# Weight slots 256 bytes longer with an offset per kind of product, and the rotary swap in the common temporaries

## The chip, the cores and the metric

The kernel runs on one core of one Trainium2 chip. The metric is device time in microseconds (us) of one execution. Before the change it takes 2052.59 us, the median of three runs (2052.55 to 2052.70).

## The reference

A decoder trunk of two layers over 512 positions and a width of 2,048, in float32: first an attention layer with compressed, selected and sliding-window keys (NSA, 16 heads of 128 in 4 key groups), then a gated linear recurrence (HGRN2, 16 heads of 128). Each layer is

```
h = rmsnorm(x, norm_w[layer])
proj = h @ w_in                      # all inputs of the mixer, and z
x = x + (mixer(proj) * silu(z)) @ w_out
```

and a last RMSNorm follows. Queries and three kinds of keys get a rotary embedding on the first 32 of 128 dimensions:

```
rot = concat([t1 * cos - t2 * sin, t2 * cos + t1 * sin])   # 16 + 16 dimensions
```

The input projections are 2,048 by 7,216 in the first layer and 2,048 by 8,192 in the second; both output projections are 2,048 by 2,048.

## The kernel before

Every large product is done in three matmuls: each operand is split into a rounded high part (fp32r) and the rest, and high x high, high x low and low x high are summed in PSUM. `split` (L75) does it: ScalarE (ACT) writes the high part, VectorE (DVE) subtracts it from the value. The normed input, transposed, stays in SBUF as `hhi` and `hlo`: 128 partitions by 16 tiles (kt) of 512 positions. Weights are loaded from HBM as `raw` tiles of 128 x 1,024 floats (three buffers) by SyncE's queue and split into `whi` and `wlo` slots of 128 x 512 floats (2,048 bytes per partition, four buffers each) by `split_weights` (L86).

Five kinds of product use them. A matmul has an operand that is loaded into the array first (the weight load, PEld in the profile) and one that streams through it (PE):

- `proj` (L102): 128 columns of weights are loaded, `hhi` or `hlo` streams with 512 positions; 48 matmuls for each of 92 calls, L110 to L112.
- `proj_pair` (L115): two such projections in two halves of 256 positions; the second one's weights go into slots with the tags `ohi` and `olo`. Called twice.
- `proj_rows` (L134): `hhi` and `hlo` are loaded, weights stream with 256 columns, L156 to L158.
- `out_proj` (L161): the split mixer output (`ohi`, `olo`, four buffers each) is loaded, weights stream with 512 columns, L176 to L178.
- `out_proj_half` (L182): the same with 256 columns, L196 to L198.

The last output projection (`last_out_proj`, L388) keeps its weights in `hhi` and `hlo` and streams them. `gates` (L497) has one small projection of its own with `whi` slots.

Tiles come from pools. Where they lie in SBUF follows from the order of the pools and from the tiles' sizes: first `consts` (with x_all, hhi, hlo, eps, ident, nw, four tiles of 16 floats and `gw`), then `weights` (raw, whi, wlo, ohi, olo), then `work`, and behind these the tiles of each layer. A tile with a tag takes the next of that tag's buffers and waits until the tile that was there has been read for the last time. `rope` (L433) copies a projection out of PSUM into a tile with the tag `tmp` (three buffers, shared with the normed rows, the z gates and others), and works on its first 32 partitions with a second tile `sw`, which has a buffer of its own: a shuffle of 32 partitions by 16, two products, and a sum, all on DVE, 28 times in all (16 queries, 12 keys). The order of instructions on each engine is set by a planner that runs a timeline of its own over the program. The PSUM accumulators of the products rotate through two banks.

Of the kernel before, what the change touches and what calls it, by code (L numbers as in the profile page):

```python
# [9 lines left out]
F32 = mybir.dt.float32  # L10
F32R = mybir.dt.float32r
# [7 lines left out]
S = 512  # L19
# [32 lines left out]
class Trunk:  # L52
# [25 lines left out]
        eng = self.nc.gpsimd if on_pool else self.nc.vector  # L78
        eng.tensor_tensor(out=lo, in0=x, in1=hi.bitcast(F32), op=ALU.subtract)  # L79

    def load_split(self, ap, shape, tags=("whi", "wlo"), share=False):
        raw = self.wpool.tile(shape, F32, name="raw", tag="raw")
        self.nc.sync.dma_start(raw, ap)
        return self.split_weights(raw, tags, share)

    def split_weights(self, raw, tags=("whi", "wlo"), share=False):  # L86

        _, nk, cols = raw.shape
        parts, step = [], 512 // cols
        for k0 in range(0, nk, step):  # L90
            n = min(step, nk - k0)
            hi, lo = (self.wpool.tile([128, n, cols], F32R, name=t, tag=t, bufs=4) for t in tags)
            self.split(raw[:, k0:k0 + n, :], hi, lo, share and k0)
            parts += [(hi[:, k, :], lo[:, k, :]) for k in range(n)]
        return parts
# [19 lines left out]
    def proj_pair(self, w, ca, cb):  # L115

        mm = self.nc.tensor.matmul
        units = []
        for c0, tags in ((ca, ("whi", "wlo")), (cb, ("ohi", "olo"))):
            parts = []  # L120
            for c in range(2):
                src = w[c * 1024:(c + 1) * 1024, c0:c0 + 128].rearrange("(k p) n -> p k n", p=128)
                parts += self.load_split(src, [128, 8, 128], tags)
            units.append((self.pproj.tile([128, S], F32, name="acc", tag="acc"), parts))
        for half in range(2):
            ts = slice(half * 256, (half + 1) * 256)
            for acc, parts in units:
                for kt, (hi, lo) in enumerate(parts):
                    mm(acc[:, ts], hi, self.hhi[:, kt, ts], start=kt == 0, stop=False)
                    mm(acc[:, ts], hi, self.hlo[:, kt, ts], start=False, stop=False)  # L130
                    mm(acc[:, ts], lo, self.hhi[:, kt, ts], start=False, stop=kt == KT - 1)
        return units[0][0], units[1][0]

    def proj_rows(self, w, c0, c1):  # L134

        accs = [self.pproj.tile([128, S], F32, name="acc", tag="acc").rearrange("p (t n) -> p t n", t=2)
                for _ in range(2)]
        for c in range(2):
            parts = []
            for r0 in range(c * 1024, (c + 1) * 1024, 512):  # L140
                raw = self.wpool.tile([128, 4, 2, 128], F32, name="raw", tag="raw")
                if c1 == c0 + 128:
                    src = w[r0:r0 + 512, c0:c0 + 256].rearrange("(k p) (b n) -> p k b n", p=128, b=2)
                    self.nc.sync.dma_start(raw, src)
                else:
                    for b, cb in enumerate((c0, c1)):
                        self.nc.sync.dma_start(raw[:, :, b, :],
                                               w[r0:r0 + 512, cb:cb + 128].rearrange("(k p) n -> p k n", p=128))
                parts += self.split_weights(raw.rearrange("p k b n -> p k (b n)"))
            for i, acc in enumerate(accs):  # L150
                for k, (hi, lo) in enumerate(parts):
                    kt = c * 8 + k
                    first, last = kt == 0, kt == KT - 1
                    for t in range(2):
                        ts = slice((2 * i + t) * 128, (2 * i + t + 1) * 128)
                        self.nc.tensor.matmul(acc[:, t, :], self.hhi[:, kt, ts], hi, start=first and t == 0, stop=False)  # L156
                        self.nc.tensor.matmul(acc[:, t, :], self.hhi[:, kt, ts], lo, start=False, stop=False)  # L157
                        self.nc.tensor.matmul(acc[:, t, :], self.hlo[:, kt, ts], hi, start=False, stop=last and t == 1)  # L158
        return [acc.rearrange("p t (b n) -> p t b n", b=2) for acc in accs]
# [22 lines left out]
    def out_proj_half(self, w, h0, og, tiles, then):  # L182

        nc = self.nc
        n = len(og)
        for e in range(8):
            es = slice(e * 256, (e + 1) * 256)
            src = w[h0 * 128:(h0 + n) * 128, es].rearrange("(k p) n -> p k n", p=128)
            parts = self.load_split(src, [128, n, 256], share=True)
            for t0 in tiles[::2]:  # L190
                acc = self.pproj.tile([128, S], F32, name="acc", tag="acc").rearrange("p (t n) -> p t n", t=2)
                for t in range(2):
                    ts = slice((t0 + t) * 128, (t0 + t + 1) * 128)
                    for k, (hi, lo) in enumerate(parts):
                        ohi, olo = (o[:, ts] for o in og[k])
                        nc.tensor.matmul(acc[:, t, :], ohi, hi, start=k == 0, stop=False)  # L196
                        nc.tensor.matmul(acc[:, t, :], ohi, lo, start=False, stop=False)
                        nc.tensor.matmul(acc[:, t, :], olo, hi, start=False, stop=k == n - 1)  # L198
                xs = self.x_all[:, t0:t0 + 2, es]
                nc.vector.tensor_tensor(out=xs, in0=acc, in1=xs, op=ALU.add)  # L200
                if e % 2:
                    then(t0, e // 2)
                    then(t0 + 1, e // 2)
# [229 lines left out]
    def rope(self, acc, q):  # L433
        nc = self.nc
        nc.scalar.copy(q, acc)
        sw = self.work.tile([64, S], F32, name="sw", tag="sw", bufs=1)
        nc.vector.stream_shuffle(sw[32:], q[:32], [(i + 16) % 32 for i in range(32)])
        nc.vector.tensor_tensor(out=sw[:32], in0=sw[32:], in1=self.rt[32:64], op=ALU.mult)
        nc.vector.tensor_tensor(out=q[:32], in0=q[:32], in1=self.rt[:32], op=ALU.mult)
        nc.vector.tensor_tensor(out=q[:32], in0=q[:32], in1=sw[:32], op=ALU.add)  # L440
# [56 lines left out]
    def gates(self, w_in):  # L497

        nc = self.nc
        n = 3 * N_HEADS  # L500

        acc = self.pproj.tile([128, S], F32, name="acc", tag="acc")
        for c in range(2):
            raw = self.wpool.tile([128, 8, n], F32, name="raw", tag="raw")
            nc.sync.dma_start(raw, w_in[c * 1024:(c + 1) * 1024, NSA_GL:NSA_Z].rearrange("(k p) n -> p k n", p=128))
            for k0 in (0, 4):
                w = self.wpool.tile([128, 4, 128], F32R, name="whi", tag="whi", bufs=4)
                self.split(raw[:, k0:k0 + 4, :], w[:, :, :n], w[:, :, n:2 * n])
                for k in range(4):
                    kt = c * 8 + k0 + k  # L510
                    both = lambda: nc.tensor.matmul(acc[:2 * n], w[:, k, :2 * n], self.hhi[:, kt, :],
                                                    start=kt == 0, stop=kt == KT - 1)
                    if kt == 0:
                        both()
                    nc.tensor.matmul(acc[:n], w[:, k, :n], self.hlo[:, kt, :], start=False, stop=False)
                    if kt:
                        both()
        gs = self.work.tile([128, S], F32, name="gs", tag="tmp", bufs=3)
        nc.scalar.copy(gs[:2 * n], acc[:2 * n])
        p = self.ptr.tile([128, 4, 128], F32, name="pt", tag="pt")  # L520
        for j in range(NT):
            nc.tensor.transpose(p[:, j, :2 * n], gs[:2 * n, j * 128:(j + 1) * 128], self.ident[:2 * n, :2 * n])
        nc.vector.tensor_copy(self.gate, p[:, :, :n])
        nc.vector.tensor_tensor(out=self.gate, in0=self.gate, in1=p[:, :, n:2 * n], op=ALU.add)
        nc.scalar.activation(self.gate, self.gate, AF.Sigmoid)
# [206 lines left out]
    def lower_bounds(self, tmp):  # L732

        nc, pool = self.nc, self.consts
# [5 lines left out]
        nc.vector.tensor_tensor(out=e, in0=e, in1=r, op=ALU.mult)  # L740
        nc.vector.tensor_tensor(out=self.lb, in0=e, in1=e, op=ALU.subtract)
        nc.vector.tensor_scalar(self.oml, self.lb, -1.0, 1.0, op0=ALU.mult, op1=ALU.add)
        self.gw = pool.tile([128, 1], F32, name="gw")
        nc.sync.dma_start(self.gw, self.hgrn_gnorm_w.rearrange("l p -> p l"))

    def level_tiles(self, pool):
# [302 lines left out]
```

## Time and profile before

| | |
|---|---|
| median of 3 runs | 2052.59 us |
| the profiled execution | 2051.99 us, of which span 2050.0 us |
| PE, PEld busy | 2019.4 us (99%), 1761.0 us (86%) |
| DVE, ACT, POOL busy | 1252.3 us (61%), 892.0 us (44%), 79.2 us (4%) |
| matmuls | 11,410 |
| the load queue of weights | 29.9% of 16 engines' time |

The span is that of one execution on the chip. PE is TensorE's matmuls and PEld its weight loads, which lie beside the matmuls. A row of a group shows the mean duration of one instruction; matmuls are pipelined, so one's duration reaches into the next, and the pace is read from the starts in the timeline.

### The profile page before, as it was taken

What the parts mean: (1) busy time and instruction counts of PE and PEld (TensorE: products, weight loads), DVE (VectorE), ACT (ScalarE), POOL (GpSimd) and SP (SyncE); (2) the same over time, 40 slices, a digit from 0 to 9 for tenths busy, and PEclk for the clock granted to TensorE, in tenths of its full rate; (3) what the DMA queues carried; (4) which work ended last, traced back from release to release, by engine and by line L of the source; (5) the groups of instructions that cost most, each with busy time, mean ns of one, the idle gap of its engine ahead of it and who ended that gap; (6) DMA issues with size and microseconds to landing.
All of it is one profiled execution on the core that took longest, in us unless ns stands there. A gap on an engine that the chain in (4) does not pass through costs nothing.

```text
span 2050.0 us, 29987 instructions
## 1 busy us (share of the span) xinstructions
PE 2019.4 (99%) x11410; PEld 1761.0 (86%) x11410; DVE 1252.3 (61%) x2944; ACT 892.0 (44%) x1966; POOL 79.2 (4%) x63
## 2 busy tenths in 40 slices
PE   7999999999999999999999999999999999999997
PEld 7789889888988889888998989789897898978885
DVE  7634676565757565756874757457574565645755
ACT  5323554444535353445743444334342344423454
POOL 5000000000000000001300000000000000000004
PEclk9999999999999999999999999999999999999999
DMA  5354222323232323232422232232222323223233
GB/s 166 84 137 110 72 67 68 93 64 91 63 93 64 93 70 93 62 83 83 146 78 87 73 93 69 83 104 74 84 74 91 93 72 93 73 82 97 74 98 114
DMA packets 272673, 179.81 MB, mean 88 GB/s; under 512 B 8192, under 2 KB 254320, under 8 KB 272528
## 3 DMA queue, kind: packets, MB, share of 16 engines
q1 hardware_dynamic: 272528, 177.88, 29.9%
q8 instruction: 90, 1.47, 0.3%
q14 instruction: 55, 0.45, 0.1%
HBM read 173.66 MB, written 4.19 MB: 87 GB/s over the span
## 4 chain that ended last, share of the span: by engine, by line
PE 94%; DVE 3%; issue 1%; ACT 1%; DMA 0%; SPq 0%; DVEq 0%
PE acc L110 16%; PE acc L112 16%; PE acc L111 16%; PE acc L176 4%; PE acc L158 4%; PE acc L156 4%; PE acc L177 4%; PE acc L157 4%; PE acc L178 4%; PE pt L665 2%; PE lv L960 1%; PE lv L936 1%; PE sc L693 1%; PE sc L691 1%; PE ov L673 1%; PE ov L672 1%
## 5 line engine op out<-in xcount | busy, mean ns | idle before, releaser
L77 ACT CAST whi<-raw 128x512 fp32r<-128x512 f32 x612 | 375.2, 618 | 664.2 <-PE acc L111 459.6
L79 DVE TENSOR_TENSOR wlo<-raw,whi 128x512 fp32r<-128x512 f32 x592 | 409.8, 700 | 384.0 <-ACT whi L77 363.8
L112 PE MATMUL acc<-hhi,wlo 128*128 128x512 f32 x1472 | 581.4, 395 | 0.0
L110 PE MATMUL acc<-hhi,whi 128*128 128x512 f32 x1472 | 580.2, 394 | 0.0
L111 PE MATMUL acc<-hlo,whi 128*128 128x512 f32 x1472 | 578.5, 393 | 0.0
L112 PEld LDWEIGHTS acc<-hhi,wlo 128*128 128x128 f32 x1472 | 276.7, 188 | 57.8
L111 PEld LDWEIGHTS acc<-hlo,whi 128*128 128x128 f32 x1472 | 276.6, 188 | 57.5
L110 PEld LDWEIGHTS acc<-hhi,whi 128*128 128x128 f32 x1472 | 276.8, 188 | 55.9
L156 PE MATMUL acc<-whi,hhi 128*128 128x256 f32 x768 | 216.2, 283 | 0.0
L158 PE MATMUL acc<-whi,hlo 128*128 128x256 f32 x768 | 215.7, 281 | 0.0
L157 PE MATMUL acc<-wlo,hhi 128*128 128x256 f32 x768 | 215.4, 281 | 0.0
L176 PE MATMUL acc<-whi,ohi 128*128 128x512 f32 x416 | 160.7, 394 | 6.3 <-DVE zz L1009 3.9
L177 PE MATMUL acc<-wlo,ohi 128*128 128x512 f32 x416 | 163.7, 394 | 0.0
L178 PE MATMUL acc<-whi,olo 128*128 128x512 f32 x416 | 163.0, 392 | 0.0
L157 PEld LDWEIGHTS acc<-wlo,hhi 128*128 128x128 f32 x768 | 145.0, 189 | 0.2
L158 PEld LDWEIGHTS acc<-whi,hlo 128*128 128x128 f32 x768 | 144.7, 188 | 0.1
L156 PEld LDWEIGHTS acc<-whi,hhi 128*128 128x128 f32 x768 | 144.1, 188 | 0.8
L180 DVE TENSOR_TENSOR x_all<-acc,x_all 128x512 f32<-128x512 f32 x112 | 77.0, 689 | 84.9 <-PE acc L178 84.5
L176 PEld LDWEIGHTS acc<-whi,ohi 128*128 128x128 f32 x416 | 78.0, 188 | 25.0 <-DVE zz L1009 5.4
L714 ACT ACTIVATE p<-p,nm 128x512 f32<-128x512 f32 (+3 forms) x128 | 71.3, 557 | 55.9 <-DVE nm L711 55.3
L177 PEld LDWEIGHTS acc<-wlo,ohi 128*128 128x128 f32 x416 | 78.1, 188 | 17.9 <-DVE wlo L79 3.0
L178 PEld LDWEIGHTS acc<-whi,olo 128*128 128x128 f32 x416 | 78.1, 188 | 15.9
(272 smaller groups left out, 2881.1 us busy)
## 6 DMA issues: line engine op xcount, KB each, us to landing
raw<-in_hgrn_w_in_dram SPq DMA_DIRECT2D x128, 512.0 KB, 4.1
raw<-in_nsa_w_in_dram SPq DMA_DIRECT2D x96, 512.0 KB, 3.8
raw<-in_nsa_w_out_dram SPq DMA_DIRECT2D x40, 512.0 KB, 3.8
raw<-in_hgrn_w_out_dram SPq DMA_DIRECT2D x32, 512.0 KB, 3.8
raw<-in_nsa_w_in_dram SPq DMA_DIRECT2D x32, 256.0 KB, 3.4
out_dram<-x_all SPq DMA_DIRECT2D x16, 256.0 KB, 2.7
x_all<-in_x_dram SPq DMA_DIRECT2D x6, 512.0 KB, 8.8
raw<-in_nsa_ck_w_dram SPq DMA_DIRECT2D x4, 512.0 KB, 4.0
```

The costliest lines, as they stand in the source:

```text
L77: self.nc.scalar.copy(hi, x)
L79: eng.tensor_tensor(out=lo, in0=x, in1=hi.bitcast(F32), op=ALU.subtract)
L110: self.nc.tensor.matmul(acc, hi, self.hhi[:, kt, :], start=first, stop=False)
L111: self.nc.tensor.matmul(acc, hi, self.hlo[:, kt, :], start=False, stop=False)
L112: self.nc.tensor.matmul(acc, lo, self.hhi[:, kt, :], start=False, stop=last)
L156: self.nc.tensor.matmul(acc[:, t, :], self.hhi[:, kt, ts], hi, start=first and t == 0, stop=False)
L157: self.nc.tensor.matmul(acc[:, t, :], self.hhi[:, kt, ts], lo, start=False, stop=False)
L158: self.nc.tensor.matmul(acc[:, t, :], self.hlo[:, kt, ts], hi, start=False, stop=last and t == 1)
L176: nc.tensor.matmul(acc, ohi, hi, start=k == n - 1, stop=False)
L177: nc.tensor.matmul(acc, ohi, lo, start=False, stop=False)
L178: nc.tensor.matmul(acc, olo, hi, start=False, stop=k == 0)
L180: nc.vector.tensor_tensor(out=xs, in0=acc, in1=xs, op=ALU.add)
```

## The change

`gw` becomes a view of a tile of 17 floats instead of 1. The slots of the tags `whi` and `wlo` become 64 floats (256 bytes) longer, and a product can place its weights some floats behind the slot's start: 16 floats in `proj_pair`, 48 in `proj_rows` and `out_proj_half`, none in the others. Slots of the tags `ohi` and `olo` stay as they are, and an offset has no effect there. `sw` takes one of the three buffers of `tmp`, of which it uses the first 64 partitions.

```
-    def split_weights(self, raw, tags=("whi", "wlo"), share=False):
+    def weight_tile(self, tag, n, cols, at=0):
+
+        pad = 64 if tag[0] == "w" else 0
+        t = self.wpool.tile([128, 512 + pad], F32R, name=tag, tag=tag, bufs=4)
+        at = min(at, pad)
+        return t[:, at:at + n * cols].rearrange("p (k n) -> p k n", k=n)
+
+    def split_weights(self, raw, tags=("whi", "wlo"), share=False, at=0):
...
-            hi, lo = (self.wpool.tile([128, n, cols], F32R, name=t, tag=t, bufs=4) for t in tags)
+            hi, lo = (self.weight_tile(t, n, cols, at) for t in tags)
...
     def proj_pair(self, w, ca, cb):
-                parts += self.load_split(src, [128, 8, 128], tags)
+                parts += self.load_split(src, [128, 8, 128], tags, at=16)
     def proj_rows(self, w, c0, c1):
-                parts += self.split_weights(raw.rearrange("p k b n -> p k (b n)"))
+                parts += self.split_weights(raw.rearrange("p k b n -> p k (b n)"), at=48)
     def out_proj_half(self, w, h0, og, tiles, then):
-            parts = self.load_split(src, [128, n, 256], share=True)
+            parts = self.load_split(src, [128, n, 256], share=True, at=48)
     def rope(self, acc, q):
-        sw = self.work.tile([64, S], F32, name="sw", tag="sw", bufs=1)
+        sw = self.work.tile([128, S], F32, name="sw", tag="tmp", bufs=3)[:64]
     def gates(self, w_in):
-                w = self.wpool.tile([128, 4, 128], F32R, name="whi", tag="whi", bufs=4)
+                w = self.weight_tile("whi", 4, 128)
     def lower_bounds(self, tmp):
-        self.gw = pool.tile([128, 1], F32, name="gw")
+        self.gw = pool.tile([128, 17], F32, name="gw")[:, :1]
```

## Rows read from the trace of the kernel before

**Rows 1.** The page, parts 1 and 2: busy time of the engines, PE's clock in tenths.

```profile
PE 2019.4 (99%) x11410; PEld 1761.0 (86%) x11410; DVE 1252.3 (61%) x2944; ACT 892.0 (44%) x1966; POOL 79.2 (4%) x63
...
PEclk9999999999999999999999999999999999999999
```

**Rows 2.** The page, part 4: shares of the chain that ended last.

```profile
PE 94%; DVE 3%; issue 1%; ACT 1%; DMA 0%; SPq 0%; DVEq 0%
```

**Rows 3.** Waits of PE, first two of eleven: us in total, times, longest.

```profile
PE pt L220 <- DMA nwrows<-in_norm_w_dram: 7.1, 1, 7.1
PE acc L176 <- DVE zz L1009: 3.9, 4, 1.3
```

**Rows 4.** The page, part 5: one line of three of `proj` and `proj_rows`.

```profile
L110 PE MATMUL acc<-hhi,whi 128*128 128x512 f32 x1472 | 580.2, 394 | 0.0
...
L156 PE MATMUL acc<-whi,hhi 128*128 128x256 f32 x768 | 216.2, 283 | 0.0
```

**Rows 5.** Timeline: start us, duration us, instruction; a matmul and the weight load beside it.

```profile
816.62 0.39 PE L176 MATMUL acc<-whi,ohi 128*128 128x512 f32 x1
816.62 0.19 PEld L177 LDWEIGHTS acc<-wlo,ohi 128*128 128x128 f32 x1
```

**Rows 6.** Timeline of PE, `proj`: the first and last of 38 starts.

```profile
582.69 0.39 PE L112 MATMUL acc<-hhi,wlo 128*128 128x512 f32 x1
...
591.16 0.39 PE L110 MATMUL acc<-hhi,whi 128*128 128x512 f32 x1
```

**Rows 7.** Timeline of PE, `last_out_proj`: the first and last of 19 starts.

```profile
2029.79 0.39 PE L406 MATMUL acc<-hhi,olo 128*128 128x512 f32 x1
...
2033.91 0.39 PE L406 MATMUL acc<-hhi,olo 128*128 128x512 f32 x1
```

**Rows 8.** Timeline of PE, `out_proj`: 8 starts to the second row, 30 from there.

```profile
1330.16 0.39 PE L178 MATMUL acc<-whi,olo 128*128 128x512 f32 x1
...
1331.78 0.39 PE L178 MATMUL acc<-whi,olo 128*128 128x512 f32 x1
...
1338.36 0.39 PE L178 MATMUL acc<-whi,olo 128*128 128x512 f32 x1
```

**Rows 9.** Timeline of PE, `proj_pair`: the first and last of 62 starts.

```profile
1018.73 0.28 PE L129 MATMUL acc<-hhi,whi 128*128 128x256 f32 x1
...
1025.91 0.28 PE L130 MATMUL acc<-hlo,ohi 128*128 128x256 f32 x1
```

**Rows 10.** Timeline of PE, `out_proj_half`: the first and last of 19 starts.

```profile
997.76 0.28 PE L196 MATMUL acc<-whi,ohi 128*128 128x256 f32 x1
...
999.92 0.28 PE L197 MATMUL acc<-wlo,ohi 128*128 128x256 f32 x1
```

**Rows 11.** Timeline of PE, `proj_rows`: two stretches, of 85 and of 64 starts.

```profile
165.09 0.28 PE L156 MATMUL acc<-whi,hhi 128*128 128x256 f32 x1
...
174.99 0.28 PE L156 MATMUL acc<-whi,hhi 128*128 128x256 f32 x1
...
344.80 0.28 PE L157 MATMUL acc<-wlo,hhi 128*128 128x256 f32 x1
...
351.94 0.28 PE L157 MATMUL acc<-wlo,hhi 128*128 128x256 f32 x1
```

**Rows 12.** Timeline of PE, `proj` right after `out_proj`: the first and last of 8 starts.

```profile
468.55 0.40 PE L110 MATMUL acc<-hhi,whi 128*128 128x512 f32 x1
...
470.17 0.39 PE L111 MATMUL acc<-hlo,whi 128*128 128x512 f32 x1
```

**Rows 13.** Pieces of the chain of waits: start us, us; short fp32 products.

```profile
105.50 5.35 PE pt L488 x48
...
252.74 0.88 PE pt L665 x8
```

**Rows 14.** The tile `sw`: a shuffle's duration (min/median/max ns), and who waited (us, times).

```profile
L437 DVE STREAM_SHUFFLE sw<-qr x16: 720/722/734, 200.1 to 903.6; 32x512 f32<-32x512 f32 x16
...
  ACT qhi L77: 10.1, 7
```

More of the change, by code (lines that the diff above doesn't have):

```diff
@@ L79, in split, with load_split @@
         eng.tensor_tensor(out=lo, in0=x, in1=hi.bitcast(F32), op=ALU.subtract)
-    def load_split(self, ap, shape, tags=("whi", "wlo"), share=False):
+    def load_split(self, ap, shape, tags=("whi", "wlo"), share=False, at=0):
         raw = self.wpool.tile(shape, F32, name="raw", tag="raw")
         self.nc.sync.dma_start(raw, ap)
-        return self.split_weights(raw, tags, share)
-    def split_weights(self, raw, tags=("whi", "wlo"), share=False):
+        return self.split_weights(raw, tags, share, at)
+    def weight_tile(self, tag, n, cols, at=0):
[4 more added lines that the diff above has]
+    def split_weights(self, raw, tags=("whi", "wlo"), share=False, at=0):
         _, nk, cols = raw.shape
```

## The prediction

> **What bounds the kernel now.** I read the page's engine shares first. [...] Of the waits of PE, the largest is the first load, 7.1 us, and the largest one after it only 3.9 us in four pieces; all eleven kinds of wait together are 20.7 us [rows 3]. The groups by line say what PE does: three lines of 1,472 matmuls in the plain projections and three of 768 in the row-wise ones [rows 4]; the output projection has, by its loops, three of 416 (six calls of 64 and one of 32).
>
> So time can only come from the distance between one matmul's start and the next. The "mean ns" of a group doesn't show that (394 ns for 512 columns overlaps the neighbour). I took it from the timeline: two starts of one uninterrupted stream, and the number of rows between. [...] What runs beside each matmul is the load of the next one's stationary weights, which starts with it: 816.62 for both [rows 5].
>
> Now the point of the case. Streams of one shape don't run at one pace. I sorted them by the place of their operands in SBUF, worked out from the tile sizes in the code (each rounded up to 32 bytes, pools in order): hhi and hlo 32,768 each, eps 32, ident 512, nw 128, four of 64, gw 32, three raw of 4,096. The first weight slot so lies 78,784 bytes behind hhi, which is 192 more than a multiple of 256. Call "distance" the start of the operand that is being loaded, minus the start of the one that streams, modulo 256:
>
> - Plain projections (hhi streams, weights are loaded), distance 192: 582.69 to 591.16 in 37 steps, 228.9 ns [rows 6].
> - Last output projection (hhi streams, ohi is loaded), also 192 with quite other code: 2029.79 to 2033.91 in 18 steps, 228.9 ns [rows 7].
> - Output projection (weights stream, ohi is loaded; both slot kinds lie 2,048 apart), distance 0: 1331.78 to 1338.36 in 29 steps, 226.9 ns [rows 8].
> - 256 columns: proj_pair, distance 192, 1018.73 to 1025.91 in 61 steps, 117.7 ns [rows 9]; out_proj_half, distance 0, 997.76 to 999.92 in 18 steps, 120.0 ns [rows 10]; proj_rows, distance 64, two steady paces, 344.80 to 351.94 in 63 steps at 113.3 ns, and 165.09 to 174.99 in 84 steps at 117.9 ns [rows 11].
>
> The pace does not depend on which k, slot or engine activity goes with it: within a kind, offsets that differ by 512 bytes give the same intervals through the whole timeline, and intervals with DVE, ACT or DMA busy differ from those without by under 1 ns on average (my sort of all starts). The best distance is thus 0 at 512 columns and 64 at 256.
>
> [...]
>
> **The change part by part.** gw becomes 17 floats, 96 bytes rounded instead of 32: everything behind it moves by 64. Slots become 2,304 bytes, nine times 256. The first slot is then 78,848 bytes behind hhi, a multiple of 256, and so is every whi, wlo, ohi and olo slot.
>
> *Plain projections*: distance 192 becomes 0. 4,416 matmuls by 228.9 - 226.9 = 2.0 ns: 8.8 us less. Not all of it stays. After an interruption, or a change from another kind, both need about seven matmuls to settle and take 231.4 ns each there: 468.55 to 470.17 at distance 192 [rows 12], 1330.16 to 1331.78 at distance 0 [rows 8]. Above their steady pace that is 7 x 2.5 = 17 ns against 7 x 4.5 = 31 ns, so each of the 187 uninterrupted stretches that I counted gives back 14 ns, 2.6 us. Left: 6.2 us. Bounds: 8.8 if settling costs nothing more, 3.0 if each stretch costs twice what is seen.
>
> *out_proj_half*: weights move by 64 + 192, distance 0 becomes 64, the pace from 120.0 to between 113.3 and 117.9. 384 matmuls by 2.1 to 6.7 ns: 0.8 to 2.6 us, I take the middle, 1.7.
>
> *proj_pair*: the whi half of 384 goes from 192 to 64 (192 x (117.7 - 115.6) = 0.4 us less), the ohi half, which has no pad, to 0 (192 x 2.3 = 0.4 us more). Zero.
>
> *proj_rows*: 64 before, and 64 after (hhi stays, the weights move by 64 + 192 = 256). Zero, but which of the two paces a stretch falls into depends on how it starts, and the starts shift. About half of the 2,304 matmuls run at either pace now; all at 113.3 would be 5.3 us less, all at 117.9 5.3 us more. I take a third of either as the spread.
>
> *Output projection, last one, gates*: the first stays at 0; the last (96 matmuls, 192 to 0) and the gates (32) give 0.2 us.
>
> *Attention and the HGRN inner part*: their tiles all move by 64 together, so distances stay. Only the transposes against ident don't move as one. They are among the short fp32 products, whose steps in the chain are 0.88 us for 8 and 5.35 us for 48, 110 and 111.5 ns [rows 13]; some 560 transposes moving within that: under 1 us either way. Zero taken.
>
> *Rotary swap*: sw now rotates through the three common temporaries, two of them per rope. Nothing is added on DVE: the 28 shuffles stay at 0.72 us [rows 14]. A new wait could only be for the tile used three allocations ago; its readers (ACT's split and DVE's subtraction, 0.6 and 0.7 us) ran at least one projection earlier, 48 x 229 ns = 11 us. That projection is the cover. Without it, each of 28 ropes would come up to 1.3 us late and hold ACT's next copy and DVE's queue behind it, up to 36 us if PE had no other work; I take zero. The other direction: DVE saved nothing, since sw with one buffer was freed in order on the same engine.
>
> *Raw tiles*: they move by 64 bytes too; the load queue takes 30% of the engines' time, and no weight load is among the waits of PE. Zero.
>
> **Sum.** 6.2 + 1.7 + 0.2 = 8.1 us of PE time. 94% of the chain is PE, so 7.6 us on the path. The profiled execution took 2051.99 us (span 2050.0 and 1.99 around it), 0.6 below the median of 2052.59: 2044.4 in its terms, **2045.0** against the median. The forecast's own range is 2041 to 2049.
>
> **The rivals.**
> 1. *The place of operands sets nothing*; the two paces belong to the code around them. [...] Against it: rows 6 and 7 share only the distance. 2052.6, no change.
> 2. *The period is 512, not 256.* Every distance at 512 columns that I could sort is a multiple of 512 apart within its kind, so 256 and 0 have never been told apart. The odd slots now lie 256 off. If those stay at 228.9, half of the projections' gain goes: 2052.6 - 4.1 = 2048.5.
> 3. *The other side: the odd slots are worse than anything now.* A tile boundary comes every 12 matmuls (4 k by 3); if odd slots keep the unsettled 231.4 ns, half of 4,416 lose 2.5 and the other half gain nothing, because they settle anew: +5.5 us. The output projection, at 0 today, loses 4.5 on half of 1,248: +2.8. proj_rows at 120.0 in half of 2,304: +5.1. With 1.7 from out_proj_half gone, 2052.6 + 13 = 2066. It decides from the point where odd slots run above 228.9 + 2.0.
> 4. *The temporaries change the order of the first layer's work.* The planner places instructions by when tiles come free; with two of three temporaries per rope, z and query copies could be placed later. Half of what ACT's query split waits for ropes today, 10.1 us [rows 14], reaching PE: +5, less the gain, 2050; with no gain 2058.
>
> **How the numbers follow.** Forecast 0.62; rival 1 0.12; rival 2 0.14; rival 3 0.08; rival 4 0.04. A change under 0.2% (4.1 us) can't be told from none. Faster: 0.56 of the forecast and 0.08 of rival 2, 0.64. Same: 0.06 + 0.12 + 0.06 = 0.24. Slower: 0.12. The range that holds 8 in 10 starts at 2040.5 (proj_rows falling well) and takes in rivals 1 and 2: 2040.5 to 2053.
>
> **What would show it.** In the timeline after: plain projections at 227 ns in steady stretches and not in the repeating 226, 229, 232 of now; out_proj_half at 113 or 118 instead of 120; the ohi half of proj_pair at 120; shuffles with no new wait before them. Wrong would be 229 unchanged (rival 1), a pace that alternates with the slot every 12 matmuls (rivals 2 and 3), or new waits of ACT and DVE at the ropes (rival 4).

## The result and the profile after

The changed kernel takes 2064.07 us (median of 4 runs, 2063.24 to 2065.72) against 2052.57 us before in the same comparison (4 runs): a ratio of 1.0058, interval 1.0046 to 1.0071. It is 11.5 us slower; 2045.0 was forecast. Its profiled execution took 2065.72 us, 13.7 more than that of before. That one is used below wherever a time is split up.

Parts 1 and 4 of the page after, beside [rows 1] and [rows 2]: PE's busy time is the same to the tenth, its share of the chain a point lower.

```profile
PE 2019.4 (98%) x11410; PEld 1764.9 (86%) x11410; DVE 1254.1 (61%) x2944; ACT 892.9 (43%) x1966; POOL 79.5 (4%) x63
...
PE 93%; DVE 4%; ACT 1%; issue 1%; DMA 0%; SPq 0%; DVEq 0%; ACTq 0%
```

The waits of PE after (us in total, times, longest), beside [rows 3]. The first line is new: three waits for ACT's copy of a key projection out of PSUM, the first instruction of `rope`. So is the last one shown, a single wait for ACT's copy of a query. The two lines of [rows 3] are still there, within 0.1 us.

```profile
PE acc L163 <- ACT kr L442: 10.2, 3, 4.1
PE pt L227 <- DMA nwrows<-in_norm_w_dram: 7.2, 1, 7.2
PE acc L183 <- DVE zz L1016: 3.9, 4, 1.3
...
PE acc L117 <- ACT qr L442: 1.0, 1, 1.0
```

The place of the three waits, in the timeline after (start us, duration us, instruction, and in brackets the idle time before it and what ended it). Read it from the bottom up: PE resumes at 350.44 when ACT's copy of `kr` has freed the PSUM bank; that copy waited for DVE's `olo`, the last reader of the two z tiles; `olo` waited for the product of z with the attention's output `o`, and `o` for the last matmuls of the attention.

```profile
346.04 0.28 PE L680 MATMUL ov<-plo,vhi 128*128 128x256 f32 x1
346.36 0.37 ACT L71 COPY o<-ov 128x256 f32<-128x256 f32 x1 [1.56 <-PE ov L680]
346.76 0.42 DVE L73 COPY o<-ov 128x256 f32<-128x256 f32 x1 [1.24 <-ACT o L71]
347.10 1.28 DVE L629 TENSOR_TENSOR zs<-o,zs 128x512 f32<-128x512 f32 x2
347.82 1.22 ACT L77 CAST ohi<-zs 128x512 fp32r<-128x512 f32 x2 [1.09 <-DVE zs L629]
348.47 1.29 DVE L79 TENSOR_TENSOR olo<-zs,ohi 128x512 fp32r<-128x512 f32 x2
349.69 0.01 DVE L444 LOAD_MASK_SELECT sw<-kr  x1
349.80 0.58 ACT L442 COPY kr<-acc 128x512 f32<-128x512 f32 x1 [0.76 <-DVE olo L79]
349.80 0.71 DVE L444 STREAM_SHUFFLE sw<-kr 32x512 f32<-32x512 f32 x1
350.44 0.58 PE L163 MATMUL acc<-whi,hhi 128*128 128x256 f32 x1 [4.11 <-ACT kr L442]
350.81 0.41 PE L164 MATMUL acc<-wlo,hhi 128*128 128x256 f32 x1
351.03 0.41 PE L165 MATMUL acc<-whi,hlo 128*128 128x256 f32 x1
```

What held the tiles, in two earlier rows of ACT in the same timeline: the second of the two z tiles is written at 300.48 and so lives for 49 us, and the first key of the group is copied at 312.07. The shuffle of that first key is the one at 349.80 above, 37 us after its copy.

```profile
300.48 0.60 ACT L635 ACTIVATE zs<-acc 128x512 f32<-128x512 f32 x1
...
312.07 0.58 ACT L442 COPY kr<-acc 128x512 f32<-128x512 f32 x1
```

Before, both keys of that group were copied inside the attention, ahead of the z product at 342.89 (timeline of before, ACT and DVE):

```profile
324.16 0.58 ACT L435 COPY kr<-acc 128x512 f32<-128x512 f32 x1
...
338.12 0.59 ACT L435 COPY kr<-acc 128x512 f32<-128x512 f32 x1
...
342.89 1.28 DVE L622 TENSOR_TENSOR zs<-o,zs 128x512 f32<-128x512 f32 x2
```

Two z tiles and one key fill the three temporaries. Before, that was just enough, since `sw` had its own buffer: the second key, copied at 338.12 while both z tiles were still to be read, can only have taken the buffer that the first key had left. So a tile doesn't always take the next buffer in turn, as the section on the kernel before has it, but one that is free. After, the first key's `sw` takes the buffer of the first z, and everything behind it on DVE and ACT follows the attention instead of running beside it. No matmul starts between 346.04 and 350.44, and none for 3.34 us from 568.32 and 3.33 us from 789.55, at the start of each of the last three key groups: 11.1 us in all.

The stalls have a second price. Stretches of the trace after and of the third experiment, which has no such stall (busy us and count of PE, PEld, DVE, ACT, POOL, then PE's granted clock, DMA share, GB/s):

```profile
346.00:353.00 7.00, 2.89 (x15) 2.68 (x14) 5.91 (x12) 2.51 (x5) 0.00 (x0) 0.57 0.00 0
...
567.00:572.00 5.00, 1.94 (x17) 1.74 (x16) 3.86 (x8) 2.18 (x4) 0.00 (x0) 1.00 0.00 0
572.00:576.00 4.00, 4.00 (x24) 4.00 (x23) 3.72 (x7) 1.14 (x2) 0.00 (x0) 0.57 0.00 0
```

```profile
346.00:353.00 7.00, 7.00 (x62) 7.00 (x62) 4.80 (x10) 2.95 (x6) 0.00 (x0) 1.00 0.48 131
```

After each stall the granted clock is at a lower level (0.50 from 573 to 575, 1.00 from 576 to 577) for some 3.4 us with PE busy: from 572 to 576 it is 0.57 on average with PE busy throughout, and the matmuls with 256 columns start 0.21 to 0.22 us apart (350.81, 351.03) instead of 0.118. In 3.4 us at 0.214 us a step PE does what takes 1.9 us at 0.118, so each stall costs another 1.5 us, three times 4.6 us. The stalls, less one ordinary step each, are 10.7 us; stalls and clock are 15.3 us.

The other side of the account is the paces. First and last start of an uninterrupted stretch of `proj_rows` (150 steps, 117.8 ns; [rows 11] had 117.9 and 113.3), of `out_proj_half` (26 steps, 113.8 ns, other stretches 117.7; [rows 10] had 120.0) and of `proj` (131 steps, 226.7 ns; [rows 6] had 228.9), in the timeline after:

```profile
169.33 0.28 PE L165 MATMUL acc<-whi,hlo 128*128 128x256 f32 x1
...
187.00 0.28 PE L165 MATMUL acc<-whi,hlo 128*128 128x256 f32 x1
...
1008.97 0.28 PE L203 MATMUL acc<-whi,ohi 128*128 128x256 f32 x1
...
1011.93 0.28 PE L203 MATMUL acc<-whi,ohi 128*128 128x256 f32 x1
...
1860.86 0.39 PE L117 MATMUL acc<-hhi,whi 128*128 128x512 f32 x1
...
1890.56 0.39 PE L119 MATMUL acc<-hhi,wlo 128*128 128x512 f32 x1
```

Over all of its starts `proj` is 6.4 us shorter in total, `out_proj_half` about 1.4 and the last output projection 0.2; `proj_rows` loses 2.5 and `proj_pair` 0.1 by their mean steps at a granted clock of 1.00, `proj_rows` because more of its stretches run at 117.8.

### The profile page after: what moved, and what is told of

Read it like the earlier page. It is cut to its first block, busy times and chain, and to the rows that moved or that the text cites. A ratio compares the mean times of both kernels' runs of the same rounds, so it can differ in the third digit from the quotient of the medians.

```text
span 2063.8 us, 29980 instructions
## 1 busy us (share of the span) xinstructions
PE 2019.4 (98%) x11410; PEld 1764.9 (86%) x11410; DVE 1254.1 (61%) x2944; ACT 892.9 (43%) x1966; POOL 79.5 (4%) x63
## 3 DMA queue, kind: packets, MB, share of 16 engines
q1 hardware_dynamic: 272528, 177.88, 29.7%
## 4 chain that ended last, share of the span: by engine, by line
PE 93%; DVE 4%; ACT 1%; issue 1%; DMA 0%; SPq 0%; DVEq 0%; ACTq 0%
PE acc L118 16%; PE acc L117 16%; PE acc L119 16%; PE acc L163 4%; PE acc L165 4%; PE acc L164 4%; PE acc L183 4%; PE acc L184 4%; PE acc L185 4%; PE pt L672 2%; PE lv L967 1%; PE lv L943 1%; PE ov L680 1%; PE sc L699 1%; PE sc L700 1%
## 5 line engine op out<-in xcount | busy, mean ns | idle before, releaser
L163 PE MATMUL acc<-whi,hhi 128*128 128x256 f32 x768 | 219.8, 288 | 10.2 <-ACT kr L442 10.2
```

## The experiments

My theory after the result: `sw` in the common temporaries costs the stalls, by the number of buffers; the offsets give what was forecast. The rivals: the places of the operands cost the time themselves, or the planner's new order does so whatever the number of buffers. Beside the first four experiments the kernel before took 2052.04 us (median of 25 runs).

**The swap alone** (the kernel before, one line):

```
-        sw = self.work.tile([64, S], F32, name="sw", tag="sw", bufs=1)
+        sw = self.work.tile([128, S], F32, name="sw", tag="tmp", bufs=3)[:64]
```

> The kernel before with one edit: sw in the common temporaries; slots and gw as they were. Theory T (temporaries): the z tiles of two heads are made early and stay in two of the three temporaries until their attention is done, so the next group's first key copy, which needs the third, and its sw, which needs a fourth, come after the attention instead of inside it; PE then waits for ACT's copy of kr. After the change this showed as 11.2 us of waits of PE (10.2 in three pieces) plus stretches at the lower clock, and the places of the weights gave back 6.4 us (7.2 + 1.3 + 0.1 less, 2.3 more in proj_rows). So without the places: 2064.1 + 6.4 = 2070 (2066 to 2074), the plain projections at 229, three waits of some 3 us each for kr. Rival P (the longer slots or their places cause the stall): 2052.6, no wait for kr.

2071.49 us (4 runs; ratio 1.0096, 1.0079 to 1.0112), as theory T has it: 19.5 slower, more than the whole change. The waits of PE have the line of the changed kernel:

```profile
PE acc L156 <- ACT kr L435: 10.3, 3, 4.1
```

There are gaps of 4.4, 3.4 and 3.4 us in the matmuls, with the lower clock behind each (granted 0.54 on average from 350 to 357, 0.80 from 570 to 578, 0.86 from 791 to 799). `proj` keeps its pace of before, 229.3 ns on average. The swap is the loss, not the offsets.

Where it is lost is read from the starts of the same two projections in both traces, before (first two lines) and with the swap (last two):

```profile
255.51 0.39 PE L110 MATMUL acc<-hhi,whi 128*128 128x512 f32 x1
...
360.32 0.39 PE L110 MATMUL acc<-hhi,whi 128*128 128x512 f32 x1
```

```profile
255.88 0.39 PE L110 MATMUL acc<-hhi,whi 128*128 128x512 f32 x1
...
370.55 0.39 PE L110 MATMUL acc<-hhi,whi 128*128 128x512 f32 x1
```

The trace with the swap is 0.4 us late at the first and 10.2 at the second, 15.2 behind the next key group's start (576.74 against 591.99) and 20.3 behind the last one's (793.18 against 813.47). So the three starts cost 9.9, 5.0 and 5.0 us. Stall and clock make up nearly all of the 5.0; in the 9.9 they are some 6.3 (an estimate from a gap of 4.4 us and 4.4 us of work at the lower clock), and a wait for a query's copy is 1.0. The other 2.5 us there belong to no wait that the trace names.

**The same with a fourth temporary** (`sw` as above; `bufs=4` wherever the tag `tmp` is):

```
-        sw = self.work.tile([64, S], F32, name="sw", tag="sw", bufs=1)
+        sw = self.work.tile([128, S], F32, name="sw", tag="tmp", bufs=4)[:64]
```

> The kernel before with sw in the common temporaries, and four of these instead of three (the same bytes as three and an sw of its own). Theory T: four are enough for two z tiles, a key and its sw, so the wait of PE for kr is gone and the time is 2052.6 within 2 us. Rival O (what costs is that sw rotates with other tiles at all, or the order the planner then chooses, not the number of buffers): 2060 or more, with waits for kr or qr.

2053.43 us (10 runs; ratio 1.0008, 0.9998 to 1.0017): no difference that can be told. No wait for `kr` is left; the first two lines of PE's waits are those of [rows 3]:

```profile
PE pt L220 <- DMA nwrows<-in_norm_w_dram: 6.8, 1, 6.8
PE acc L176 <- DVE zz L1009: 3.9, 4, 1.3
```

The second of the two projections above starts at 360.58 instead of 360.32, and the trace stays 0.3 us behind that of before up to 1,010 us, past the whole attention:

```profile
360.58 0.39 PE L110 MATMUL acc<-hhi,whi 128*128 128x512 f32 x1
```

So it isn't the sharing as such that costs, but that three buffers don't hold two z tiles, a key and its `sw`.

**The change with another place for `sw` of the keys** (the changed kernel; eight of the 28 ropes, those of the attention's keys, take `sw` from the buffers of the queries' low parts):

```
...
-                    self.rope(acc, k)
+                    self.rope(acc, k, self.att.tile([128, S], F32R, name="sw", tag="qlo").bitcast(F32)[:64])
```

> The kernel after, but the ropes of the eight attention keys take their sw from the buffers of qlo (free between the groups) instead of the common temporaries; the places of the weights as in the change. Theory T: the stall at the start of groups 1 to 3 is gone and the gain of the places stays: 2052.6 less 6.4 us, 2046 (2043 to 2050), plain projections at 227. Rival P (slots or places cause the stall): near 2064 still.

2049.52 us (10 runs; ratio 0.9988, 0.9979 to 0.9998). Taking `sw` of the eight keys out of the temporaries so gives back 14.6 us (2064.07 - 2049.52; 16.5 between the two profiled executions, of which 15.3 are the stalls and the clock counted above). No wait for `kr` is left; the one for a query's copy, 1.0 us at 283, is. It came out 3.5 us short of the 2046 expected. The 6.4 us in it held 2.3 us for `proj_rows` already, which now loses 3.0 (117.0 ns on average against 115.7 before), and 7.2 for `proj`, which gives 6.4. The largest part is again at the first key group's start. The same two projections as above start 1.4 us earlier than before and then 1.1 us later:

```profile
254.06 0.39 PE L117 MATMUL acc<-hhi,whi 128*128 128x512 f32 x1
...
361.41 0.39 PE L117 MATMUL acc<-hhi,whi 128*128 128x512 f32 x1
```

Of these 2.5 us the query's wait is 1.0.

**The small tile alone** (the kernel before with `gw` of 17 floats: everything behind it moves by 64 bytes, no slot is longer, and the order of the instructions is that of before):

```
-        self.gw = pool.tile([128, 1], F32, name="gw")
+        self.gw = pool.tile([128, 17], F32, name="gw")[:, :1]
```

> The kernel before with gw as a view of 17 floats and nothing else: all that lies behind gw moves by 64 bytes, slots stay 2,048 apart, no offsets, sw as before, the order of instructions unchanged. Theory D (the distance modulo 256 of the operand loaded from the one that streams sets the pace): plain projections at distance 0, 226.7 ns settled (7 us less); proj_rows at distance 0, 120 ns instead of 115.7 on average (2,304 x 4.3 = 9.9 us more); proj_pair at 120 instead of 117.7 (0.9 more); out_proj_half stays at 120. Sum 3.6 us slower, 2056 (2054 to 2058). Rival (distance sets nothing by itself, the longer slots do): 2052.6, paces 229, 115.7 and 117.7.

2054.04 us (10 runs; ratio 1.0011, 1.0001 to 1.0020), at the low end of the range expected. All kinds are now at distance 0. Timeline: `proj_rows` 151 steps, 120.0 ns (113.3 or 117.9 before); `proj` 131 steps, 226.6 ns.

```profile
168.53 0.28 PE L157 MATMUL acc<-wlo,hhi 128*128 128x256 f32 x1
...
186.65 0.28 PE L158 MATMUL acc<-whi,hlo 128*128 128x256 f32 x1
...
1847.70 0.39 PE L110 MATMUL acc<-hhi,whi 128*128 128x512 f32 x1
...
1877.39 0.39 PE L112 MATMUL acc<-hhi,wlo 128*128 128x512 f32 x1
```

Over all of their starts: `proj` -6.3 us, `proj_rows` +8.7, `proj_pair` +0.7, the last output projection -0.2: +2.9 together, measured +2.0. One edit of 64 bytes moves two kinds in opposite directions, with the same instructions in the same order. `out_proj` and `out_proj_half`, whose two operands both moved by the 64 bytes, keep their settled paces, 227.3 and 120.0 ns. So it is the distance of the two operands, not where they lie. Other tiles behind `gw` moved as well; the scans below move the weights alone.

**Two scans of the distance** (the third experiment, with the offset different from call to call; the first in steps of 32 bytes for `proj` and 16 for `proj_rows`, the second finer; the first varied `out_proj_half` too, which is not read here):

```
-        return self.load_split(src, [128, 8, 128])
+        return self.load_split(src, [128, 8, 128], at=8 * (c0 // 128 % 8))
...
+        at = (0, 0, 1, 63, 2, 62, 4, 60)[c0 // 128 % 8]
```

> The repaired kernel (e3) with the offset of the weights varied by call, to read the settled pace at many distances from one trace: proj by head in steps of 8 floats (distances 0, 32, ... 224), proj_rows from 32 to 60 floats (distances 128 down to 16 in steps of 16), out_proj_half from 0 to 60 floats in steps of 4. Theory D (distance modulo 256 sets the pace): proj 226.7 at 0 and 228.9 at 192 as measured, other steps between 215.8 and 233; proj_rows at 64 with its two paces 113.3 and 117.8, at 0 120; some distance near 64 may have 113.3 as its only pace. Rival (only multiples of 64 differ, by halves of a 128-byte line): steps of 16 and 32 give the pace of the nearest multiple of 64. The total says little: near 2050.

> A second reading of distances in the repaired kernel: proj_rows by call at 28 and 8 floats (distances 144 and 224), at 46, 47, 49, 50 floats (72, 68, 60, 56), proj at 0, 1, 2, 4, 60, 62 and 63 floats (0, 4, 8, 16, 240, 248, 252). Theory D with a step finer than a multiple of 64: next to 0 and next to 64 the paces worsen at once, to between 228 and 233 in proj and 116 to 120 in proj_rows, and no distance beats 226.7 and 113.3. Rival (the distance is taken in lines of some bytes, so that a few floats more change nothing): 4 and 8 bytes off give 226.7 and the pair 113.3/117.8 as at 0 and 64; then the offsets need not be exact. From the first scan, 144 and 224 in proj_rows: 113 to 118. The total says little: 2055 to 2070.

2071.65 and 2064.27 us (one run each; before beside them 2051.44 and 2052.85). The first total was not the 2050 that I expected, because nearly every distance is worse than those that the kernels use. The rivals of both scans fall, as steps of 4 and of 32 bytes have paces of their own; theory D's upper bounds, 233 and 120 ns, were a little low, and its lower one at 512 columns, 215.8 ns, no run shows: the lowest mean step read is 226.6. Mean steps (ns) after the first nine of each stretch:

| distance, bytes | `proj`, 512 columns | distance, bytes | `proj_rows`, 256 columns |
|---|---|---|---|
| 0 | 226.7 | 0 (fourth experiment) | 120.0 |
| 4 / 252 | 232.4 / 233.3 | 56, 60 | 120.3, 120.8 |
| 8 / 248 | 230.7 / 233.3 | 64 | 113.3 or 117.8 |
| 16 / 240 | 226.7 or 233.4 / 227.9 | 68, 72 | 119.2, 120.0 |
| 32 to 160 | 232.8 to 234.3 | 16 to 48, 80 to 128 | 117.2 to 119.3 |
| 192 | 229.3 | 144 | 113.4 |
| 224 | 233.3 | 224 | 116.8 |

Two stretches of `proj` in the timelines, 32 bytes off (first scan, 131 steps, 233.3 ns) and 4 bytes off (second scan, 46 steps, 232.2 ns):

```profile
1608.67 0.39 PE L117 MATMUL acc<-hhi,whi 128*128 128x512 f32 x1
...
1639.23 0.40 PE L119 MATMUL acc<-hhi,wlo 128*128 128x512 f32 x1
```

```profile
53.49 0.39 PE L119 MATMUL acc<-hhi,whi 128*128 128x512 f32 x1
...
64.17 0.40 PE L120 MATMUL acc<-hlo,whi 128*128 128x512 f32 x1
```

Four bytes cost 5.7 ns of each matmul. At 64 bytes `proj_rows` has two paces; at 144 it has the faster one alone.

**144 bytes for the products with 256 columns** (the third experiment with three other offsets):

```
-                parts += self.load_split(src, [128, 8, 128], tags, at=16)
+                parts += self.load_split(src, [128, 8, 128], tags, at=36)
-                parts += self.split_weights(raw.rearrange("p k b n -> p k (b n)"), at=48)
+                parts += self.split_weights(raw.rearrange("p k b n -> p k (b n)"), at=28)
-            parts = self.load_split(src, [128, n, 256], share=True, at=48)
+            parts = self.load_split(src, [128, n, 256], share=True, at=28)
```

> The changed kernel with sw of the key ropes in the qlo buffers, as in the third experiment (2049.5), and the offsets of the products with 256 columns set so that the loaded operand lies 144 bytes (modulo 256) from the streaming one: 28 floats in proj_rows and out_proj_half, 36 in proj_pair. If the pace is set by the distance alone and 144 bytes has one pace there: proj_rows from 117.0 to about 114.7 ns, 2304 x 2.3 = 5.3 us less, out_proj_half and the whi half of proj_pair 0.3 us less each: 2043.6 (2041 to 2047), no wait for kr. If the pace at 144 bytes is as much a matter of how a stretch starts as at 64: 2049.5 (2047 to 2052).

2045.57 us (5 runs; ratio 0.9964, 0.9951 to 0.9978): 6.8 us faster than before, the fastest kernel here. `proj_rows` in the timeline, the stretch that ran at 117.8 ns in the changed kernel, now 149 steps of 113.3:

```profile
171.24 0.28 PE L163 MATMUL acc<-whi,hhi 128*128 128x256 f32 x1
...
188.12 0.28 PE L165 MATMUL acc<-whi,hlo 128*128 128x256 f32 x1
```

It came 2 us short of the 2043.6 expected: `proj_rows` averaged 115.2 ns, its settled steps 113.5 but the first nine of each stretch 117.5, and for `proj_pair` 144 is no good place (119.4 ns against 116.3 at 64 bytes).

That last number also says that the distance isn't the whole rule. At 144 bytes `proj_rows` and `out_proj_half` settle at 113.5 and 114.0 ns, `proj_pair`, with the same 256 columns, at 119.4. In `proj_pair` the weights are the operand that is loaded, in the other two the one that streams; whether that makes the difference was not tested.

## Why the prediction was wrong

The step that failed is the one on the rotary swap: "A new wait could only be for the tile used three allocations ago; its readers (ACT's split and DVE's subtraction, 0.6 and 0.7 us) ran at least one projection earlier, 48 x 229 ns = 11 us. That projection is the cover." Three allocations ahead of the first key's `sw` of a group stands no tile of a rope but the first of the two z tiles (then come the second z and the key itself). I gave it the readers of a rope's tile, as if only ropes used the temporaries. The z tiles share them, are written before the attention that they gate has ended (300.48) and are last read behind it (`olo`, until 349.76). So the last reader did not run one projection earlier: it ended 37 us after the key had been copied, and there was no cover. The rows were at hand: in the trace of before the z product at 342.89 stands behind both key copies.

The price was wrong with it. I bounded a missing cover by 1.3 us for each of 28 ropes. In fact three of them cost 5.1 us each (15.3 / 3): PE stands still until the attention's last products are done, then works at the lower clock (0.50 granted). Of the other 25 a wait of PE of 1.0 us is seen.

- *Plain projections*: right. 6.2 us forecast, 6.4 measured, settling included; steady steps 228.9 to 226.7.
- *out_proj_half*: 1.7 forecast, 1.4 measured. *proj_pair*, zero: +0.1. *Last projection and gates*, 0.2: 0.2.
- *proj_rows*: zero taken, "a third of either as the spread" (1.8 us). It was +2.5, and +3.0 without the stalls, outside that spread but within the 5.3 that bounded it. At 64 bytes a stretch runs at 113.3 or at 117.8 ns; what decides it stays open. The last experiment shows the way round.
- *Raw tiles, attention, transposes*: nothing of theirs appears; the load queue has 29.7% against 29.9%, and in the third experiment the attention's steps differ by 0.4 us in all from those of before.
- *Waits of PE before*: the eleven rows add up to 20.9 us, not 20.7; nothing hangs on it.

Of the rivals, 1 falls with the fourth experiment. The scans say the same: `proj` steps by 226.7 ns at distance 0 and by 233.3 at 224, with nothing moved but the weights. What in the chip makes the difference, no run here shows. Rivals 2 and 3 fall with the changed kernel itself: its slots lie 2,304 bytes apart, so they are 0 and 256 modulo 512 in turn, and odd and even ones both step by 226.7 ns. Rival 4 named the place, the first layer's order, and sized it by ACT's waits at query splits. Those grew only from 10.1 to 13.8 us ([rows 14] before); the loss came through the keys, whose copy out of PSUM frees the bank that PE needs (10.2 us of waits for `kr`). I gave it 0.04 and 2050 or 2058; with 15.3 us in place of its 5 it would have said 2060.

The sum in the profiled executions: 15.3 of stalls and clock, 1.0 for the query's wait, and -5.4 by the paces (-6.4 - 1.4 - 0.2 + 2.5 + 0.1) give +10.9 against +13.7 measured. The 2.8 us that are missing fit the 2.5 that the swap alone leaves without a wait at the first key group's start; the third experiment, which leaves the queries' `sw` in the temporaries, keeps about 1.3 of them there (2.5 less 1.0 for the query's wait and an estimated 0.2 by the paces). That is part of why the swap alone costs more (19.5) than the repair gives back (14.6). What causes these 2.5 us stays open.

## What to carry to other kernels

When a tile moves into a shared rotating buffer, list every user of that tag with the time from its first write to its last read, and count how many live at once; which allocation stood there before says nothing until its last reader is placed in time. Where ScalarE or VectorE waits, look which PSUM bank the waiting copy frees, and whether PE has other work: here three such copies held PE for 10.2 us. Where streams of one shape run at different paces, sort them by the address of the loaded operand minus that of the streaming one, and scan this distance for each kind of product: here the best for 512 columns (226.7 ns at 0) was among the worst for 256 (120.0), and at 144 bytes two kinds with 256 columns differed by 6 ns (113.4 and 119.4).

## What the hardware showed

- The step of these fp32r matmuls, with a weight load each, went with that distance: 226.7 to 234.3 ns at 512 columns, 113.3 to 120.8 at 256. Slots 256 bytes apart modulo 512 gave one pace (226.7). Of the distances read, 0 is the best at 512 columns and close to the worst at 256 (120.0). It isn't the whole rule: at 144 bytes `proj_rows` has 113.4 ns and `proj_pair` 119.4.
- It is sharp: 4 bytes off 0 give 232.4 or 233.3 ns, 4 bytes off 64 give 120.8 or 119.2. Some distances have two paces (64 at 256 columns, 16 at 512).
- PE's granted clock fell from 1.00 to 0.50 in or shortly after each stall of 3.3 to 4.4 us, and PE worked some 3.4 us at it (0.57 on average from 572 to 576), so each stall cost another 1.5 us. In the second experiment it fell at 1036 with no single wait of PE above 1.1 us ahead of it: PE was busy 3.19 of the 5 us from 1031 to 1036 (granted 1.00), and 0.57 was granted from 1036 to 1040. The page's clock row in tenths of 40 slices shows 9 throughout, after as before [rows 1], because a slice is 51.6 us long.
